# Hybrid decoder step, convolution stage: SiLU as one ScalarE function per group of four tiles, z in the last group, norms issued later

## The chip, the cores and the metric

The kernel runs on one core of one Trainium2 chip. The metric is device time in microseconds (us) of one execution; lower is better. The core has TensorE (PE, matmuls; its weight loads are listed as PEld), VectorE (DVE), ScalarE (ACT), GpSimd (POOL) and SyncE (SP, which issues most DMAs). Each engine works through its own instructions in order, and they wait for each other through semaphores.

## The reference, cut to what matters

One layer of a decoder on 256 prompt rows and 32 sample rows (288 in all). The normalised input is multiplied by `w_in`; the columns feed two attention mixers and a gated DeltaNet (mixer B). The change is in mixer B: a causal depthwise convolution of width 4 with SiLU on q, k and v, a normalisation of q and k, and a SiLU gate z at the output.

```python
def delta_branch(b_qkv, b_z, b_beta, b_alpha, conv_buf, s0, conv_w, a_log, dt_bias, dn_g):
    full = jnp.concatenate([conv_buf.astype(b_qkv.dtype), b_qkv], axis=1)
    conv = sum(full[:, j:j + L] * conv_w[j] for j in range(CONV_W))
    conv = jax.nn.silu(conv).astype(jnp.float32).reshape(n, L, 3, B_HEADS, B_HEAD_DIM)
    q = l2_normalize(conv[:, :, 0]) * (B_HEAD_DIM ** -0.5)
    k = l2_normalize(conv[:, :, 1])
    v = conv[:, :, 2]
    ...
    o, s_new = gated_delta_chunked(q, k, v, g, beta, s0)
    o = rms_norm(o, dn_g) * jax.nn.silu(b_z.astype(jnp.float32).reshape(n, L, B_HEADS, B_HEAD_DIM))
```

Then `x + norm(mix @ w_out)`, and an MLP with `w_up` and `w_down`.

## The kernel before, in words

Activations lie transposed: features on the 128 partitions, the 288 rows along the free axis. Every weight matrix is a stream of **pieces**, in a fixed order: 88 of `w_in` and one small one (`w_ba`), 32 of `w_out`'s first part (o1), 8 of its second (o2), then the MLP's. A `w_in` piece is 128x1024, that is eight 128x128 blocks; two pieces make one unit of 128 output columns. fp32 accuracy is had from three FP32R products: the weight is split into a high half `wh` and a low half `wl`, the activation into `xh` and `xl`, and each block costs three matmuls of 288 columns (`run_mats`, L447, all recorded at L307), so 24 for a `w_in` piece and 18 for an o1 piece (six blocks). Per piece SP loads the raw weight `wr`, ACT casts it to `wh` (`split_to`, L366, recorded at L375), and DVE subtracts `wl = wr - wh` (`low_to`, L385, recorded at L317). For a piece with the mark `gp`, set at L1381 for six pieces of mixer B, POOL does that subtraction. Casts are issued four pieces ahead of the matmuls, subtractions three, loads six; there are four buffers each of `wr`, `wh` and `wl`.

The last 24 pieces of `w_in` give the twelve **convolution tiles** m = 0 to 11 (0-3 are q, 4-7 k, 8-11 v; one tile per head). The four z units come before them and wait in `mixp[:, 6:10, :]` (`base_mix` in the profile). When a tile's matmuls are done, `conv_tile` (L615) scales the accumulator into `cv_zb` with two DVE instructions. Then a generator `g_conv` (L640) is stepped: ACT multiplies by the first tap and DVE adds three taps (all writing `cv_ca`), and SiLU is built from Exp and Ln without changing the activation table. `silu_a` or L653 clamps (DVE, writes `cv_e`), `silu_e` does Exp, Ln, Exp (ACT, `cv_e` and `cv_s`), `silu_b` does two DVE instructions (`cv_e`, `cv_s`) and a product on POOL into `cv_ca`. For q and k there follows a norm: ACT squares (`cv_sq`), PE sums over partitions with a matrix of ones (`ps_lx<-cv_sq`), ACT takes Ln and Exp (`cv_nr`) and a square, DVE makes the scale with two instructions (`cv_sq`), and POOL multiplies by `cv_nr` and by the scale (`b_k`, `b_qD`, `b_kD`). For v, PE transposes the tile (`ps_mx<-base_cst,cv_ca`) and ACT copies it to `b_vt`. `cv_sq` and `cv_nr` have two buffers each.

Such side work is woven between the matmuls. Each piece is cut in four, and after each cut `advance` (L487) steps every generator that is ready by an estimated PE clock; a generator yields how much PE time has to pass before its next step. `drain` (L514) forces a generator to its end. So the order on every engine is fixed when the program is built. `g_silu_z` (L575) makes the SiLU of the four z tiles after all convolution tiles. `g_gate` makes the decay gates (`cv_gc`, `cv_gd`, `cv_bD`, `cv_gD`). `g_chunk` (L813, two chunks of 128 rows) waits for tiles 0-7, computes `b_cA`, `b_cB`, `b_cU` from k and q, and inverts a triangular matrix by levels (`inverse`, L763: `b_cN`, `b_cM`, `b_cAA`); these products run among the o1 pieces. `g_bfin` ends the mixer before the o2 pieces. At the start of o1, `split_mix` splits twelve finished rows of the mix (ACT casts `base_xh<-base_mix`, DVE subtractions `base_xl`).

Of the kernel before, what the change touches and what calls it, by code (L numbers as in the profile page):

```python
# [7 lines left out]
AF = mybir.ActivationFunctionType  # L8
ALU = mybir.AluOpType
# [4 lines left out]
P = 128  # L14
# [3 lines left out]
T = TP + TS  # L18
# [221 lines left out]
def build(tc, d):  # L240
    nc = tc.nc
    PE, V, S, G, SP = nc.tensor, nc.vector, nc.scalar, nc.gpsimd, nc.sync
# [23 lines left out]
    def mx(n=512, p=P):  # L266
        return ps.t([P, 512], "mx", 4)[0:p, 0:n]
# [17 lines left out]
    dng = pm[:, 112:113]  # L285
# [23 lines left out]
    def tr(out, in_, idn):  # L309
        clk[0] += max(in_.shape[0], in_.free_size()) / 600.0  # L310
        PE.transpose(out, in_, idn)  # L311

    def act(out, in_, func, **kw):
        S.activation(out=out, in_=in_, func=func, **kw)  # L314

    def tt(eng, out, a, b, op):
        eng.tensor_tensor(out=out, in0=a, in1=b, op=op)  # L317

    def ts(eng, out, a, s1, op0, s2=None, op1=None):
        if op1 is None:  # L320
            eng.tensor_scalar(out=out, in0=a, scalar1=s1, scalar2=None, op0=op0)
        else:
            eng.tensor_scalar(out=out, in0=a, scalar1=s1, scalar2=s2, op0=op0, op1=op1)

    def stt(eng, out, a, s, b, op0, op1, **kw):
        eng.scalar_tensor_tensor(out=out, in0=a, scalar=s, in1=b, op0=op0, op1=op1, **kw)  # L326
# [25 lines left out]
    pieces = []  # L352
# [161 lines left out]
    def drain(*names):  # L514
        guard = 0
        while any(n not in done for n in names):
            for name in [g[1] for g in sorted(gens, key=lambda g: g[2])]:
                if guard % 6 < 5 and name not in names:
                    continue
                for i in range(len(gens)):  # L520
                    if gens[i][1] == name:
                        step(i)
                        break
                if all(n in done for n in names):
                    return
            guard += 1
            assert guard < 5000, (names, [g[1] for g in gens])
# [30 lines left out]
    def open_b():  # L558
        bp.open("b", "right")
        cv.open("cv")  # L560
        cvp["buf"] = cv.t([P, 12, 24], "cbuf")
        cvp["co"] = cv.t([P, 12, 27], "convo")
        SP.dma_start(out=cvp["buf"], in_=d["cbuf"])
        B["k"], B["q"] = (bp.t([P, 4, TP], "k4", 2) for _ in range(2))
        B["vt"] = bp.t([P, 2, 4, P], "vt")
        B["kD"], B["qD"], B["vD"] = (bp.t([P, P], t) for t in ("kD", "qD", "vD"))
        B["o"] = bp.t([P, 4, T], "oB")
        add_gen(g_silu_z(), "siluz", 6.0)
        add_gen(g_gate(), "gate")
# [5 lines left out]
    def g_silu_z():  # L575
        for h in range(4):
            z = mixp[:, 6 + h, :]
            while not all(f"cs{m}" in done for m in range(12)):
                yield 3.0
            e, q = silu_a(cv, z, T)  # L580
            yield 2.0
            silu_e(e, q)
            yield 4.0
            silu_b(e, q, z, G)
            yield 2.5
            act(z, z, AF.Identity, scale=dng)
            yield 1.0

    def maybe_close_cv():
        if "sp" not in done and all(n in done for n in ["siluz", "gate", "convout"] + [f"conv{m}" for m in range(12)]):  # L590
# [5 lines left out]
    def silu_a(pool, x, w):
        e = pool.t([P, ZW], "e", 3)
        s = pool.t([P, ZW], "s", 3)
        ts(V, e[:, :w], x, -80.0, ALU.max)
        return e[:, :w], s[:, :w]  # L600

    def silu_e(e, s):
        act(e, e, AF.Exp, scale=-1.0)
        act(s, e, AF.Ln, bias=1.0, scale=1.0)
        act(s, s, AF.Exp, scale=-1.0)

    def silu_b(e, s, x, eng):
        stt(V, e, e, 1.0, s, ALU.add, ALU.mult)
        stt(V, s, e, 2.0, s, ALU.subtract, ALU.mult, reverse0=True)
        tt(eng, x, x, s, ALU.mult)  # L610

    def decv(ap):
        return ap[:, 259:315].rearrange("p (n s) -> p n s", s=7)[:, :, 0:4]

    def conv_tile(m, acc):  # L615
        if m >= 4:
            drain(f"conv{m - 4}")
        if m >= 3:
            drain(f"cz{m - 3}")
        zb = cv.t([P, ZW], "zb", 3)  # L620
        G.memset(zb[:, 0:3], 0.0)
        zd = zb[:, 259:315].rearrange("p (n s) -> p n s", s=7)
        G.tensor_copy(out=zd[:, :, 0:3], in_=cvp['buf'][:, m, :].rearrange("p (n s) -> p n s", s=3))
        R = cur["R"]
        tt(V, zb[:, 3:259], acc[:, 0:TP], R[:, 0:TP], ALU.mult)
        tt(V, zd[:, :, 3:7], acc[:, TP:T].rearrange("p (n s) -> p n s", s=4),
           R[:, TP:T].rearrange("p (n s) -> p n s", s=4), ALU.mult)
        G.tensor_copy(out=cvp['co'][:, m, 0:3], in_=zb[:, 256:259])
        G.tensor_copy(out=cvp['co'][:, m, 3:27].rearrange("p (n s) -> p n s", s=3), in_=zd[:, :, 4:7])
        add_gen(g_conv(m, zb), f"conv{m}", 1.5, front=True)  # L630
        if m == 11:
            add_gen(g_convout(), "convout")

    def g_convout():
# [2 lines left out]
            yield 2.0  # L637
        G.dma_start(out=d["conv"], in_=cvp['co'])

    def g_conv(m, zb):  # L640
        kind, h = m // 4, m % 4
        while m >= 3 and f"cs{m - 3}" not in done:
            yield 1.0
        y = cv.t([P, ZW], "ca", 5)
        yc = y[:, :CW]
        act(yc, zb[:, 0:CW], AF.Identity, scale=convw[:, m, 0:1])
        yield LT[6]
        for j in range(1, 4):
            stt(V, yc, zb[:, j:j + CW], convw[:, m, j:j + 1], yc, ALU.mult, ALU.add)
        e = cv.t([P, ZW], "e", 3)[:, :CW]  # L650
        q = cv.t([P, ZW], "s", 3)[:, :CW]
        ts(V, e, yc, -80.0, ALU.max)
        done.add(f"cz{m}")  # L653
        yield LT[0]
        silu_e(e, q)
        yield LT[1]
        silu_b(e, q, yc, G)
        done.add(f"cs{m}")
        yield LT[2] if kind < 2 else LT[8]
        if kind < 2:  # L660
            while m >= 2 and f"cn{m - 2}" not in done:
                yield 1.0
            sq = cv.t([P, ZW], "sq", 2)
            act(sq[:, :CW], yc, AF.Square)
            yield LT[3]
            p = lx(CW)
            mm(p, ones, sq[:, :CW])
            yield LT[4]
            r = cv.t([P, CW], "nr", 2)
            act(r, p, AF.Ln, bias=epsc[:, 0:1], scale=1.0)  # L670
            act(r, r, AF.Exp, scale=-0.5)
            w = sq[:, :CW]
            act(w, r, AF.Square)
            yield LT[5]
# [11 lines left out]
            done.add(f"cn{m}")
        else:
            G.tensor_copy(out=B["vD"][:, 32 * h:32 * h + 32].rearrange("p (n s) -> p n s", s=4), in_=decv(y))
            p = mx(256)
            for c in range(2):  # L690
                tr(p[:, c * P:(c + 1) * P], y[:, c * P:(c + 1) * P], ident)
            S.copy(out=B["vt"][:, :, h, :], in_=p.rearrange("p (c n) -> p c n", c=2))
# [1188 lines left out]
```

## Time and profile before

| what | us |
|---|---|
| three runs before | 1435.38, 1436.96, 1439.16 (median 1436.96) |
| the profiled execution's own time | 1436.89 |
| its span, first to last instruction | 1435.0 |
| PE busy | 1384.9 (97%) |
| DVE busy | 823.1 (57%) |
| ACT busy | 601.8 (42%) |
| POOL busy | 177.3 (12%) |
| convolution stage: first matmul after the tile-0 pieces to the first `b_cN` x `b_cAA` product | 329.42 to 445.38 |

The page gives busy times as averages over the whole span. The stage in question is about a twelfth of it, so it has to be read with views of that stretch alone: busy time per 20 us, waits by releaser, groups by shape, and the order of time. In the view of stretches, a row gives the stretch, its length, and per engine busy us and number of instructions, then the granted clock of TensorE (1.00 is full speed) and the DMA share. In the view of groups, a row ends with total busy us, mean ns of one | idle time before them and what ended it.

### The profile page before, as it was taken

What the parts mean: (1) busy time and instruction counts of PE and PEld (TensorE: products, weight loads), DVE (VectorE), ACT (ScalarE), POOL (GpSimd) and SP (SyncE); (2) the same over time, 40 slices, a digit from 0 to 9 for tenths busy, and PEclk for the clock granted to TensorE, in tenths of its full rate; (3) what the DMA queues carried; (4) which work ended last, traced back from release to release, by engine and by line L of the source; (5) the groups of instructions that cost most, each with busy time, mean ns of one, the idle gap of its engine ahead of it and who ended that gap; (6) DMA issues with size and microseconds to landing.
All of it is one profiled execution on the core that took longest, in us unless ns stands there. A gap on an engine that the chain in (4) does not pass through costs nothing.

```text
span 1435.0 us, 25761 instructions
## 1 busy us (share of the span) xinstructions
PE 1384.9 (97%) x10685; PEld 1320.9 (92%) x10685; DVE 823.1 (57%) x1313; ACT 601.8 (42%) x943; POOL 177.3 (12%) x230
## 2 busy tenths in 40 slices
PE   7899999999999998999999999999999999999994
PEld 7688888789889998899999999999999999999994
DVE  7454455437999647977534455434555444555555
ACT  7343434435664235653433343333334333344441
POOL 2112111103861005000000000000000000000114
PEclk9999999999999999999999999999999999999997
DMA  7778888753433244645554454455554554545541
GB/s 260 271 269 328 298 320 335 272 183 117 140 93 104 88 156 132 213 162 191 179 175 162 149 175 162 162 176 163 161 169 156 175 166 158 176 158 167 172 151 66
DMA packets 70629, 262.27 MB, mean 183 GB/s; under 512 B 8080, under 2 KB 10256, under 8 KB 70512
## 3 DMA queue, kind: packets, MB, share of 16 engines
q1 hardware_dynamic: 68112, 254.94, 52.6%
q0 software_dynamic: 1536, 4.89, 0.9%
q8 instruction: 84, 1.38, 0.4%
q10 hardware_dynamic: 864, 0.80, 0.2%
q14 instruction: 33, 0.27, 0.1%
HBM read 253.35 MB, written 7.24 MB: 182 GB/s over the span
## 4 chain that ended last, share of the span: by engine, by line
PE 86%; DVE 8%; DMA 2%; issue 2%; POOL 1%; ACT 1%; POOLq 0%; SPq 0%; ACTq 0%; DVEq 0%
PE ps_mx L307 34%; PE ps_acc L307 31%; PE ps_lx L307 20%; DVE base_wl L317 2%; DVE cv_ca L326 2%; PE ps_mx L311 1%; DMA kv_kv<-kv_k 1%; POOL ml_y L317 1%; DVE base_mix L317 1%; DMA base_cst<-cst 1%; DVE cv_e L326 1%; DVE base_xl L317 1%; DVE base_xl L326 0%; DVE cv_s L326 0%; DVE cv_zb L317 0%
## 5 line engine op out<-in xcount | busy, mean ns | idle before, releaser
L375 ACT CAST base_wh<-base_wr 128x1024 fp32r<-128x1024 f32 (+1 forms) x376 | 387.0, 1031 | 566.8 <-PE ps_mx L307 207.3
L317 DVE TENSOR_TENSOR base_wl<-base_wr,base_wh 128x1024 fp32r<-128x1024 f32 (+1 forms) x369 | 449.3, 1231 | 66.3 <-ACT base_wh L375 64.4
L307 PE MATMUL ps_acc<-base_xh,base_wh 128*128 128x288 f32 (+1 forms) x1056 | 325.3, 309 | 3.4 <-ACT base_xh L1476 3.4
L307 PE MATMUL ps_acc<-base_xl,base_wh 128*128 128x288 f32 (+1 forms) x1056 | 313.7, 299 | 0.4
L307 PE MATMUL ps_acc<-base_xh,base_wl 128*128 128x288 f32 x1040 | 309.6, 298 | 0.7 <-DVE base_wl L317 0.6
L307 PEld LDWEIGHTS ps_acc<-base_xh,base_wh 128*128 128x128 f32 (+1 forms) x1056 | 199.9, 189 | 20.9 <-issue 14.6
L307 PE MATMUL ps_mx<-ml_big,base_wh 128*128 128x288 f32 x1024 | 203.3, 295 | 0.0
L307 PEld LDWEIGHTS ps_acc<-base_xl,base_wh 128*128 128x128 f32 (+1 forms) x1056 | 199.5, 189 | 2.6 <-DVE base_xl L317 1.4
L307 PEld LDWEIGHTS ps_acc<-base_xh,base_wl 128*128 128x128 f32 x1040 | 198.6, 191 | 1.5 <-DVE base_wl L317 1.4
L307 PEld LDWEIGHTS ps_mx<-ml_big,base_wh 128*128 128x128 f32 x1024 | 164.3, 188 | 0.0
L307 PE MATMUL ps_mx<-ml_big,base_wl 128*128 128x288 f32 x512 | 151.1, 295 | 0.0
L307 PE MATMUL ps_mx<-base_xh,base_wh 128*128 128x288 f32 x480 | 142.5, 297 | 0.0
L307 PE MATMUL ps_mx<-base_xl,base_wh 128*128 128x288 f32 x480 | 141.9, 296 | 0.0
L307 PE MATMUL ps_mx<-base_xh,base_wl 128*128 128x288 f32 x480 | 141.4, 295 | 0.0
L307 PE MATMUL ps_lx<-base_xh,base_wh 128*128 128x288 f32 x400 | 121.2, 304 | 6.1 <-ACT base_xh L314 6.1
L307 PE MATMUL ps_lx<-base_xh,base_wl 128*128 128x288 f32 x400 | 118.7, 297 | 3.3 <-DVE base_wl L317 3.3
L307 PE MATMUL ps_lx<-base_xl,base_wh 128*128 128x288 f32 x400 | 117.8, 298 | 0.0
L307 PE MATMUL ps_lx<-ml_big,base_wh 128*128 128x288 f32 x512 | 101.8, 295 | 0.0
L307 PE MATMUL ps_acc<-ml_big,base_wh 128*128 128x288 f32 x512 | 101.8, 295 | 0.0
L317 POOL TENSOR_TENSOR ml_sacc<-ml_sacc,ml_sq 128x288 f32<-128x288 f32 x15 | 12.8, 853 | 717.3 <-ACT ml_sq L314 717.3
L307 PEld LDWEIGHTS ps_mx<-ml_big,base_wl 128*128 128x128 f32 x512 | 96.4, 188 | 0.0
L307 PEld LDWEIGHTS ps_mx<-base_xh,base_wl 128*128 128x128 f32 x480 | 90.5, 189 | 0.0
(415 smaller groups left out, 2028.6 us busy)
## 6 DMA issues: line engine op xcount, KB each, us to landing
base_wr<-w_up SPq DMA_DIRECT2D x128, 512.0 KB, 3.5
base_wr<-w_dn SPq DMA_DIRECT2D x128, 512.0 KB, 3.5
base_wr<-w_in SPq DMA_DIRECT2D x88, 512.0 KB, 4.3
kv_kv<-kv_k SPq DMA_DIRECT2D x24, 896.0 KB, 8.3
kv_kv<-kv_v SPq DMA_DIRECT2D x28, 768.0 KB, 7.1
base_wr<-w_o SPq DMA_DIRECT2D x32, 384.0 KB, 3.1
base_wr<-w_o SPq DMA_DIRECT2D x8, 512.0 KB, 4.0
ml_big<-xT SPq DMA_DIRECT2D x4, 576.0 KB, 4.8
```

What stands on the lines that cost most here:

```text
L307: PE.matmul(out, lhsT=lhsT, rhs=rhs, start=start, stop=stop, **kw)
L311: PE.transpose(out, in_, idn)
L317: eng.tensor_tensor(out=out, in0=a, in1=b, op=op)
L326: eng.scalar_tensor_tensor(out=out, in0=a, scalar=s, in1=b, op0=op0, op1=op1, **kw)
L375: S.copy(out=p["wh"], in_=p["wr"])
```

## The change

SiLU of the convolution tiles becomes one ScalarE function (`AF.Silu`). It needs another activation table, so tiles are taken in groups of four: `g_group(kind)` waits until its four tiles have all taps added, loads the table set `silu_and_others` by name, applies Silu in place to four tiles, and loads `natural_log_exp_and_others` again. In the last group (v), one Silu over all four z tiles at once (128x1152) stands ahead of the four, and one multiplication by `dng` over 1152 columns follows; `g_silu_z` goes. The norms of a group are stepped one after the other after its Silu. The norm is written another way: ACT's third square and POOL's product with `cv_nr` go, and DVE has three scalar_tensor_tensor instead of one and a tensor_scalar. `cv_ca` has nine buffers instead of five; the buffers `cv_e` and `cv_s` go. The mark `gp` at L1381 goes, so the six low halves that POOL made are DVE's.

```diff
@@ open_b: the generator of z goes
-        add_gen(g_silu_z(), "siluz", 6.0)
         add_gen(g_gate(), "gate")
...
     def conv_tile(m, acc):
-        if m >= 4:
-            drain(f"conv{m - 4}")
+        if m >= NCA:
+            while f"conv{m - NCA}" not in done:
+                drain(f"convg{(m - NCA) // 4}")
         if m >= 3:
             drain(f"cz{m - 3}")
...
-        add_gen(g_conv(m, zb), f"conv{m}", 1.5, front=True)
+        add_gen(g_conv(m, zb), f"convt{m}", 1.5, front=True)
+        if m % 4 == 3:
+            add_gen(g_group(m // 4), f"convg{m // 4}", 1.5, front=True)
...
+    NCA = 9
+
     def g_conv(m, zb):
-        kind, h = m // 4, m % 4
-        while m >= 3 and f"cs{m - 3}" not in done:
-            yield 1.0
-        y = cv.t([P, ZW], "ca", 5)
+        y = cv.t([P, ZW], "ca", NCA)
+        cvp["y", m] = y
         yc = y[:, :CW]
         act(yc, zb[:, 0:CW], AF.Identity, scale=convw[:, m, 0:1])
         yield LT[6]
         for j in range(1, 4):
             stt(V, yc, zb[:, j:j + CW], convw[:, m, j:j + 1], yc, ALU.mult, ALU.add)
-        e = cv.t([P, ZW], "e", 3)[:, :CW]
-        q = cv.t([P, ZW], "s", 3)[:, :CW]
-        ts(V, e, yc, -80.0, ALU.max)
         done.add(f"cz{m}")
-        yield LT[0]
-        silu_e(e, q)
-        yield LT[1]
-        silu_b(e, q, yc, G)
...
+    def g_group(kind):
+        ms = range(4 * kind, 4 * kind + 4)
+        while not all(f"cz{m}" in done for m in ms):
+            yield 1.0
+        yield 1.5
+        S.preload_act_table_set("silu_and_others")
+        if kind == 2:
+            zs = mixp[:, 6:10, :]
+            act(zs, zs, AF.Silu)
+        for m in ms:
+            yc = cvp["y", m][:, :CW]
+            act(yc, yc, AF.Silu)
+        S.preload_act_table_set("natural_log_exp_and_others")
+        if kind == 2:
+            act(zs, zs, AF.Identity, scale=dng)
+            done.add("siluz")
+        yield 6.0
+        for m in ms:
...
             sq = cv.t([P, ZW], "sq", 2)
             act(sq[:, :CW], yc, AF.Square)
-            yield LT[3]
+            yield 2.5
             p = lx(CW)
             mm(p, ones, sq[:, :CW])
-            yield LT[4]
             r = cv.t([P, CW], "nr", 2)
             act(r, p, AF.Ln, bias=epsc[:, 0:1], scale=1.0)
             act(r, r, AF.Exp, scale=-0.5)
             w = sq[:, :CW]
-            act(w, r, AF.Square)
-            yield LT[5]
             sc = float(P) ** -0.5 if kind == 0 else 1.0
-            stt(V, w, p, EPS, w, ALU.add, ALU.mult)
-            ts(V, w, w, -0.5 * sc, ALU.mult, 1.5 * sc, ALU.add)
-            tt(G, yc, yc, r, ALU.mult)
-            yield LT[7]
+            stt(V, w, p, EPS, r, ALU.add, ALU.mult)
+            stt(V, w, w, -0.5 * sc, r, ALU.mult, ALU.mult)
+            stt(V, w, w, 1.5 * sc, r, ALU.add, ALU.mult)
             dp, dd = ((B["q"], B["qD"]), (B["k"], B["kD"]))[kind]
             tt(G, dp[:, h, :], y[:, 0:TP], w[:, 0:TP], ALU.mult)
...
-            pieces[-1]["gp"] = u != "ba" and UNITS[u][0] == "b" and u % 2 == 0 and h == 0
```

The change moves instructions at three places that matter below. First POOL, in the stretch where the norms of q are made (`b_k_2` here is the q buffer). Before:

```order
L317 TENSOR_TENSOR cv_ca_3929<-cv_ca_3929,cv_s_3973 128x312
L317 TENSOR_TENSOR base_wl_4062<-base_wr_3912,base_wh_4061 128x1024
L621 MEMSET cv_zb_4102 128x3
L623 COPY cv_zb_4102<-cv_cbuf_3688 128x8x3
L628 COPY cv_convo_3689<-cv_zb_4102 128x3
L629 COPY cv_convo_3689<-cv_zb_4102 128x24
L317 TENSOR_TENSOR cv_ca_3828<-cv_ca_3828,cv_nr_4074 128x312
L317 TENSOR_TENSOR b_k_2_3692<-cv_ca_3828,cv_sq_4031 128x256
L317 TENSOR_TENSOR b_qD_3695<-cv_ca_3828,cv_sq_4031 128x28
L317 TENSOR_TENSOR b_qD_3695<-cv_ca_3828,cv_sq_4031 128x4
```

POOL there after the change:

```order
L317 TENSOR_TENSOR b_k_2_3691<-cv_ca_3743,cv_sq_4148 128x256
L317 TENSOR_TENSOR b_qD_3694<-cv_ca_3743,cv_sq_4148 128x28
L317 TENSOR_TENSOR b_qD_3694<-cv_ca_3743,cv_sq_4148 128x4
L591 MEMSET cv_zb_4216 128x3
L593 COPY cv_zb_4216<-cv_cbuf_3687 128x8x3
L598 COPY cv_convo_3688<-cv_zb_4216 128x3
L599 COPY cv_convo_3688<-cv_zb_4216 128x24
```

Of POOL's work per q tile only the products with the scale and the small copies are left; the 1024-column subtraction and two 312-column products are gone.

Second, DVE in the same stretch. Before:

```order
L326 SCALAR_TENSOR_TENSOR cv_e_4081<-cv_e_4081,cv_s_4082 128x312
L326 SCALAR_TENSOR_TENSOR cv_s_4082<-cv_e_4081,cv_s_4082 128x312
L326 SCALAR_TENSOR_TENSOR cv_ca_4146<-cv_zb_4102,base_pm_62,cv_ca_4146 128x312 x3
L321 TENSOR_SCALAR cv_e_4176<-cv_ca_4146 128x312
L317 TENSOR_TENSOR cv_zb_4197<-ps_acc_4114,base_R_387 128x256
L317 TENSOR_TENSOR cv_zb_4197<-ps_acc_4114,base_R_387 128x8x4
L317 TENSOR_TENSOR base_wl_4155<-base_wr_4022,base_wh_4154 128x1024
L326 SCALAR_TENSOR_TENSOR cv_sq_4124<-ps_lx_4144,cv_sq_4124 128x312
L323 TENSOR_SCALAR cv_sq_4124<-cv_sq_4124 128x312
L317 TENSOR_TENSOR base_wl_4205<-base_wr_4066,base_wh_4204 128x1024
```

DVE there after the change:

```order
L317 TENSOR_TENSOR base_wl_4096<-base_wr_3987,base_wh_4095 128x1024
L317 TENSOR_TENSOR base_wl_4136<-base_wr_4020,base_wh_4135 128x1024
L326 SCALAR_TENSOR_TENSOR cv_sq_4148<-ps_lx_4182,cv_nr_4184 128x312
L326 SCALAR_TENSOR_TENSOR cv_sq_4148<-cv_sq_4148,cv_nr_4184 128x312 x2
L326 SCALAR_TENSOR_TENSOR cv_ca_4162<-cv_zb_4128,base_pm_62,cv_ca_4162 128x312 x3
L317 TENSOR_TENSOR cv_zb_4216<-ps_acc_4141,base_R_387 128x256
L317 TENSOR_TENSOR cv_zb_4216<-ps_acc_4141,base_R_387 128x8x4
L317 TENSOR_TENSOR base_wl_4171<-base_wr_4066,base_wh_4170 128x1024
```

The clamp and the two SiLU instructions are gone, the norm has three instructions, and every piece's low half stands here. Norms now follow each other every 24 weight matmuls instead of every 48, and the first four begin five tiles later.

Third, ACT among the first o1 pieces, where the last group lies. `b_cT` belongs to the second chunk's gates, `b_vt` are the transposed v tiles, `b_cAA` the copies for the inversion. Before:

```order
L314 ACTIVATE b_cT_27_4827<-b_cT_27_4827 128x512
L692 COPY b_vt_3693<-ps_mx_4904 128x2x128
L375 CAST base_wh_4908<-base_wr_4756 128x768
L314 ACTIVATE cv_e_4883<-cv_e_4883 128x312
L314 ACTIVATE cv_s_4884<-cv_e_4883 128x312
L314 ACTIVATE cv_s_4884<-cv_s_4884 128x312
L375 CAST base_wh_4956<-base_wr_4833 128x768
L692 COPY b_vt_3693<-ps_mx_5000 128x2x128
L771 COPY b_cAA_32_5010<-ps_mx_5013 128x512
```

ACT there after the change:

```order
L314 ACTIVATE b_cT_27_4733<-b_cT_27_4733 128x512
L375 CAST base_wh_4803<-base_wr_4660 128x768
L629 ACT_TABLE_LOAD
L314 ACTIVATE base_mix_65<-base_mix_65 128x1152
L314 ACTIVATE cv_ca_4437<-cv_ca_4437 128x312
L314 ACTIVATE cv_ca_4512<-cv_ca_4512 128x312
L314 ACTIVATE cv_ca_4605<-cv_ca_4605 128x312
L314 ACTIVATE cv_ca_4751<-cv_ca_4751 128x312
L636 ACT_TABLE_LOAD
L314 ACTIVATE base_mix_65<-base_mix_65,base_pm_62 128x1152
L375 CAST base_wh_4853<-base_wr_4739 128x768
L650 COPY b_vt_3692<-ps_mx_4897 128x2x128
```

Two table loads, five Silu and the scaling of z stand as one block between two casts, ahead of all four `b_vt` copies. SP's order is unchanged, and PE's is the same again from the first `b_cN` x `b_cAA` product on.

More of the change, by code (lines that the diff above doesn't have):

```diff
@@ L573, in open_b @@
         add_gen(g_bfin(), "bf")
[L575 to L581, printed above, removed]
-            silu_e(e, q)
[L583 to L586, printed above, removed]
-            yield 1.0
     def maybe_close_cv():
@@ L594, in maybe_close_cv @@
             done.add("sp")
[L596 to L610, printed above, removed]
     def decv(ap):
@@ L638, in g_convout @@
         G.dma_start(out=d["conv"], in_=cvp['co'])
+    NCA = 9
     def g_conv(m, zb):
-        kind, h = m // 4, m % 4
-        while m >= 3 and f"cs{m - 3}" not in done:
-            yield 1.0
-        y = cv.t([P, ZW], "ca", 5)
+        y = cv.t([P, ZW], "ca", NCA)
+        cvp["y", m] = y
         yc = y[:, :CW]
@@ L649, in g_conv @@
             stt(V, yc, zb[:, j:j + CW], convw[:, m, j:j + 1], yc, ALU.mult, ALU.add)
-        e = cv.t([P, ZW], "e", 3)[:, :CW]
-        q = cv.t([P, ZW], "s", 3)[:, :CW]
-        ts(V, e, yc, -80.0, ALU.max)
         done.add(f"cz{m}")
-        yield LT[0]
-        silu_e(e, q)
-        yield LT[1]
-        silu_b(e, q, yc, G)
[L658 to L662, printed above, removed]
+    def g_group(kind):
[16 more added lines that the diff above has]
+        for m in ms:
+            h = m % 4
+            y = cvp.pop(("y", m))
+            yc = y[:, :CW]
+            if kind == 2:
+                G.tensor_copy(out=B["vD"][:, 32 * h:32 * h + 32].rearrange("p (n s) -> p n s", s=4), in_=decv(y))
+                p = mx(256)
+                for c in range(2):
+                    tr(p[:, c * P:(c + 1) * P], y[:, c * P:(c + 1) * P], ident)
+                S.copy(out=B["vt"][:, :, h, :], in_=p.rearrange("p (c n) -> p c n", c=2))
+                done.add(f"conv{m}")
+                yield 0.7
+                continue
             sq = cv.t([P, ZW], "sq", 2)
             act(sq[:, :CW], yc, AF.Square)
-            yield LT[3]
+            yield 2.5
             p = lx(CW)
             mm(p, ones, sq[:, :CW])
-            yield LT[4]
             r = cv.t([P, CW], "nr", 2)
@@ L685, in g_conv @@
             tt(G, dv_[:, 7, :], yv[:, 7, :], sq[:, 308:312], ALU.mult)
[L686 to L692, printed above, removed]
+            done.add(f"conv{m}")
+        yield 2.5
     def g_gate():
```

## The prediction

> **What bounds the kernel now.** I read the page's totals first, then busy time per 20 us, then TensorE's waits in the stage, then the groups behind the engine that makes PE wait.
>
> ```profile
> PE 1384.9 (97%) x10685; PEld 1320.9 (92%) x10685; DVE 823.1 (57%) x1313; ACT 601.8 (42%) x943; POOL 177.3 (12%) x230
> 340.00:360.00 20.00, 18.43 (x121) 17.57 (x121) 17.55 (x35) 12.52 (x25) 11.33 (x17) 0.91 0.41 132
> 360.00:380.00 20.00, 17.88 (x119) 17.36 (x118) 19.58 (x28) 13.18 (x24) 16.79 (x23) 0.91 0.40 132
> ...
> 420.00:440.00 20.00, 18.51 (x138) 17.09 (x138) 19.72 (x45) 12.95 (x33) 5.25 (x7) 1.00 0.31 99
> ...
> 460.00:480.00 20.00, 20.00 (x169) 20.00 (x168) 14.06 (x25) 5.11 (x8) 1.34 (x2) 1.00 0.27 80
> ```
>
> PE is busy 97% of the span, so a gain has to come from the places where it is not. The convolution stage is one: PE is idle 1.5 to 2.1 us of every 20, and there DVE, 57% on average, is busy 19.6 and 19.7 of 20. At 460:480 PE is full again. The work on z before it lies at 440 to 460, so its end delays nobody; taking it away is worth nothing at that place.
>
> ```profile
> engine line waited for: us in total, times, longest us
> PE ps_lx L307 <- ACT cv_sq L314: 5.7, 3, 2.5
> PE ps_mx L307 <- POOL cv_bD L720: 1.4, 1, 1.4
> ...
> ```
>
> These are PE's waits from 329 to 446; with five more, 2.2 together and none over 0.6, they sum to 9.3. To them comes the clock: 0.91 in two stretches means 0.09 x 20 = 1.8 us lost in each, 3.6 in all. So **12.9 us** lie in this stage (a count of its matmuls at 0.133, worked out below, gives about 14.7). The largest wait is for the squares of the norm, which stand late because the chain DVE taps, SiLU, POOL product ends late.
>
> **DVE's load.** Why is DVE full?
>
> ```profile
> L326 DVE SCALAR_TENSOR_TENSOR cv_ca<-cv_zb,base_pm,cv_ca 128x312 f32<-128x312 f32 x36 | 33.1, 919 | 1.4 <-ACT cv_ca L314 0.6
> L326 DVE SCALAR_TENSOR_TENSOR cv_ca<-cv_zb,base_pm,cv_ca x36: 534/545/3023, 336.8 to 431.6; 128x312 f32<-128x312 f32 x36
> 361.99 4.33 DVE L326 SCALAR_TENSOR_TENSOR cv_ca<-cv_zb,base_pm,cv_ca 128x312 f32<-128x312 f32 x3
> 362.74 2.65 POOL L317 TENSOR_TENSOR base_wl<-base_wr,base_wh 128x1024 fp32r<-128x1024 f32 x1
> 430.43 1.70 DVE L326 SCALAR_TENSOR_TENSOR cv_ca<-cv_zb,base_pm,cv_ca 128x312 f32<-128x312 f32 x3
> ```
>
> The taps' median is 545 ns (minimum, median, maximum in the second row), their mean 919: three of them take 4.33 us while POOL subtracts a low half beside them, and 1.70 at 430.43, where POOL has nothing. So 36 x (919 - 545) = 13.5 us of DVE's time go with POOL's work beside it.
>
> **What goes and comes on DVE.**
>
> ```profile
> L326 DVE SCALAR_TENSOR_TENSOR cv_e<-cv_e,cv_s 128x312 f32<-128x312 f32 x12 | 9.5, 790 | 0.0
> L326 DVE SCALAR_TENSOR_TENSOR cv_s<-cv_e,cv_s 128x312 f32<-128x312 f32 x12 | 5.8, 485 | 0.4
> L321 DVE TENSOR_SCALAR cv_e<-cv_ca 128x312 f32<-128x312 f32 x12 | 3.9, 322 | 0.4
> L323 DVE TENSOR_SCALAR cv_sq<-cv_sq 128x312 f32<-128x312 f32 x8 | 6.5, 807 | 0.3
> L326 DVE SCALAR_TENSOR_TENSOR cv_sq<-ps_lx,cv_sq 128x312 f32<-128x312 f32 x8 | 3.8, 474 | 0.0
> L317 DVE TENSOR_TENSOR base_wl<-base_wr,base_wh 128x1024 fp32r<-128x1024 f32 x15 | 18.2, 1214 | 0.0
> ```
>
> Clamps and SiLU's two steps leave: 3.9 + 9.5 + 5.8 = 19.2. The norm goes from 0.474 + 0.807 to three of 0.474 = 1.42: plus 0.14 x 8 = 1.1. Six low halves come back: 6 x 1.21 = 7.3. Of the 13.5 most goes with POOL's low halves and SiLU products; some 2 to 3 us stay beside POOL's `b_k` products. In sum DVE loses 19.2 - 1.1 - 7.3 + 11 = about 22 us in a stage of five slices of at most 20 each. It has room again at every piece until the last group.
>
> **ACT.**
>
> ```profile
> L314 ACT ACTIVATE cv_e<-cv_e 128x312 f32<-128x312 f32 x12 | 5.6, 465 | 19.0 <-DVE cv_e L321 19.0
> L1734 ACT ACT_TABLE_LOAD x1 | 1.3, 1283 | 0.7 <-PEq L1871 0.7
> L314 ACT ACTIVATE sp_fa<-b_oB 128x1152 f32<-128x1152 f32 x1 | 1.2, 1172 | 0.0
> ```
>
> 36 functions of 0.465 become 12; eight squares go. No Silu is in this trace: the nearest rows are Exp (0.465) and the taps' Identity (0.545), and I take 0.47, by the shape of Exp. Over 1152 columns one function takes 1.17; z needs two. [...] ACT is busy 12.5 to 13.2 of 20 us in the slices above, so four of the six loads, behind which only casts issued four pieces ahead wait, cost nothing; without that cover they would cost 1.3 each. The two of the v group do not hide, as the sum shows.
>
> [...]
>
> **PE's way to the chunk's matrices.** From the first product of `b_cN` and `b_cAA` on, the orders of before and after are the same and PE is full, so what counts is when that product stands.
>
> ```profile
> 326.00 0.29 PE L307 MATMUL ps_acc<-base_xh,base_wl 128*128 128x288 f32 x1
> ...
> 329.20 0.29 PE L307 MATMUL ps_acc<-base_xh,base_wl 128*128 128x288 f32 x1
> 375.33 0.79 PE L307 MATMUL ps_lx<-cv_sq,base_cst 128*128 128x312 f32 x2 [2.12 <-ACT cv_sq L314]
> 419.03 1.95 PE L307 MATMUL ps_mx<-base_cst,b_gP 128*128 128x128 f32 x16
> 445.38 1.05 PE L307 MATMUL ps_mx<-b_cN,b_cAA 128*128 128x128 f32 x8
> ```
>
> 24 matmuls later is 3.20 us later: 0.133 each. The gate products `b_gP` stood at 419.03. Lost until then: 5.7 for `cv_sq`, 1.4 for `cv_bD` and 3.6 of clock, 10.7 in all. If nothing of it stays (the waits go with DVE's load; the half clock followed such waits), they stand at 408.3. The sum over partitions of the first k norm (tile 4) stands 72 matmuls (9.6) and four norm sums (0.7 each) ahead of them: at about 395.9. So Ln and Exp have its scale ready at about 397.5.
>
> **DVE's tail** has no gap from there, in the new order:
>
> ```profile
> 416.90 3.67 DVE L317 TENSOR_TENSOR base_xl<-base_mix,base_xh 128x288 fp32r<-128x288 f32 x8
> ...
> 422.23 0.51 DVE L317 TENSOR_TENSOR cv_zb<-ps_acc,base_R 128x256 f32<-128x256 f32 x2
> 422.66 1.56 DVE L317 TENSOR_TENSOR base_xl<-base_mix,base_xh 128x288 fp32r<-128x288 f32 x4
> 427.48 0.15 DVE L825 COPY b_gl<-ps_mx 128x4 f32<-128x4 f32 x1
> ...
> 429.56 0.95 DVE L317 TENSOR_TENSOR base_wl<-base_wr,base_wh 128x768 fp32r<-128x768 f32 x1
> 437.55 0.68 DVE L317 TENSOR_TENSOR b_cB<-ps_mx,b_cA 128x512 f32<-128x512 f32 x1
> 438.15 1.11 DVE L326 SCALAR_TENSOR_TENSOR b_cU<-ps_mx,b_bP,b_cA 128x128 f32<-128x128 f32 x4
> ```
>
> Four k norms 5.7; one low half of 1024 columns 1.2; six of 768 (0.9 to the next start) 5.4; taps of tiles 9 to 11, 5.1 and 1.0 beside `b_k`; two `cv_zb` 1.0; `base_xl` 5.2; from `b_gl` to the `wl` behind it 2.1, and 0.5 for that group's start; `b_cB` and `b_cU` twice 3.4; a copy 0.4. Sum 31.0: the second `b_cU` ends at about **428.5**, against 439.26 now.
>
> ```profile
> 428.97 1.26 ACT L314 ACTIVATE b_cA<-b_cA,b_ngc 128x128 f32<-128x128 f32 x4
> ...
> 432.94 0.35 ACT L692 COPY b_vt<-ps_mx 128x256 f32<-128x256 f32 x1
> ```
>
> ACT's leg: its work from the first `b_cA` to `b_cT` takes 4.0 us (428.97 to 432.94). Shifted with DVE's `b_cA` rows it starts at 418.8; a cast of 0.8 behind it ends at 423.6. Then load 1.28, Silu over z 1.17, Silu of tile 8 0.47: 426.5. PE stands at tile 8's transposes for about 2 us, since its in-order queue has them ahead of the transposes of `b_cU`. Both legs then end alike: PE has some 3.3 us of transposes and small products (the first behind 426.5), to 429.8; 36 matmuls (4.8) and 0.5 of small ones, and the product stands at 435.1. **Gain 10.3.** I deduct 1.3: a half clock of 1.8 after the new waits at even odds (0.9), and 0.4 for change-overs dearer than the row. So 9.0 from the profiled run's own 1436.89 (its median of three is 1436.96): **1428**; own range 1425 to 1432.
>
> The clock rows of 0.91 follow waits of only 1.4 and 2.1 us. [...]
>
> **POOL** loses 12 products and six low halves, which no PE wait names, and keeps `b_k` and `b_qD`:
>
> ```profile
> 358.49 1.58 POOL L317 TENSOR_TENSOR b_k<-cv_ca,cv_sq 128x256 f32<-128x256 f32 x1 [0.32 <-DVE cv_sq L323]
> 360.04 0.96 POOL L317 TENSOR_TENSOR b_qD<-cv_ca,cv_sq 128x28 f32<-128x28 f32 x2
> ```
>
> **The rivals.**
> *PE-bound throughout (0.13).* DVE's tail and the Silu group are shorter than I add them up, all 12.9 to 14.7 us come back: 1422 to 1424. For it: 97% PE. Against: DVE 19.72 of 20 us at 420:440, where nothing but SiLU's steps leaves.
> *A dearer tail (0.14).* [...]
> *The long taps stay (0.12).* The 13.5 us are not POOL's removed work: `b_k`, bunched, blocks DVE as much. Then DVE's load falls by only 11, the stage keeps about two thirds of its loss: gain 3 to 4, 1433. Against it: the pair at 361.99 and 362.74.
> *Slower (0.09): the norm's ring.* Norms now come one behind the other, one for about each piece (3.2 + 0.7 us), on two `cv_sq` buffers. One buffer's round is 0.45 square + 0.8 sum + 1.0 Ln and Exp + 1.4 DVE + 2.5 POOL = 6.2 us, against two slots of 7.8. It decides when DVE or POOL reaches a norm over 1.5 us late; then PE waits for `cv_sq` at each of eight norms as at 375.33, 2.1 x 8 = 17, and 5 in the tail: 22 against 14.7 lost now, +7: 1444. Against it: DVE has room there.
>
> **How the numbers follow.** The forecast has 0.52. About 0.3%, 4.3 us, is what a measurement can tell from no change, so faster means below 1432.6: 0.52 + 0.13 + 0.09 of the dearer tail = 0.74. Within: its other 0.05 and the long taps, 0.17. Slower 0.09. The range runs from the PE-bound end to the long taps, 1421.5 to 1434.5, and leaves the ring and some of each end out.
>
> **What would show it.** Right: `cv_ca` taps at a mean of 0.55 to 0.65; PE's waits for `cv_sq` under 0.5; clock 1.00 from 340 to 380; seven table loads of 1.28; the `b_cN` product at about 435; a wait of about 2 us at tile 8's transposes for ACT's `cv_ca`. From there all rows shifted alike. Wrong: `cv_sq` waits at each norm (ring); taps still near 0.9; a clock below 1.00 in 420:440; or idle in front of ACT's functions beyond the load.

## The result, and the profile after

| | before | after |
|---|---|---|
| median (runs) | 1437.43 us (4) | 1427.66 us (4) |
| lowest and highest | 1435.38 to 1439.16 | 1425.44 to 1428.06 |
| profiled execution, its span | 1436.89, 1435.0 | 1427.82, 1426.0 |

The ratio is 0.9924, with a 95% interval of 0.9912 to 0.9936: 9.8 us faster by the medians, 9.0 by the two spans. The forecast was 1428.0.

First the totals of the kernel after, and its busy time per 20 us in the stage (columns as before: stretch, length, then busy us and instructions of PE, PEld, DVE, ACT and POOL, granted clock, DMA share, GB/s).

```profile
PE 1380.8 (97%) x10685; PEld 1317.3 (92%) x10685; DVE 798.1 (56%) x1279; ACT 590.7 (41%) x903; POOL 138.7 (10%) x200
340.00:360.00 20.00, 20.00 (x153) 19.82 (x153) 14.87 (x32) 9.95 (x17) 8.35 (x14) 1.00 0.59 197
360.00:380.00 20.00, 20.00 (x147) 19.56 (x146) 14.96 (x26) 13.37 (x21) 8.72 (x16) 1.00 0.40 133
380.00:400.00 20.00, 20.00 (x149) 19.70 (x148) 16.41 (x29) 14.35 (x22) 7.69 (x18) 1.00 0.46 138
400.00:420.00 20.00, 19.14 (x138) 18.00 (x137) 19.65 (x44) 12.83 (x32) 9.95 (x20) 1.00 0.25 80
420.00:440.00 20.00, 17.70 (x140) 17.00 (x139) 16.98 (x32) 15.27 (x28) 3.62 (x7) 1.00 0.33 93
```

From 340 to 400 PE is full at full clock, and DVE has 3.6 to 5.1 us of every 20 to spare. What is left of the loss lies behind 400, in the tail: there DVE is full again, and then PE has its largest gaps, 2.3 us of 20. PE's waits from 329 to 437 in the kernel after say the same:

```profile
PE ps_lx L307 <- DVE base_wl L317: 0.8, 1, 0.8
PE ps_mx L311 <- ACT cv_ca L314: 0.8, 1, 0.8
PE ps_acc L307 <- DVE base_xl L317: 0.7, 1, 0.7
PE ps_mx L311 <- ACT b_vt L650: 0.7, 1, 0.7
PE ps_acc L307 <- DVE base_wl L317: 0.5, 1, 0.5
```

3.5 us in place of 9.3; no wait for `cv_sq` or `cv_bD`. **A measure for the stage**: runs differ by some us before it starts, since PE waits at 40 us for the DMA of `kv_k` (the longest of these waits is 5.0 us in the kernel after, and 3.7 in e9 below). So I read it between two products that every kernel here has, the gate's and the first of `b_cN` with `b_cAA`. In order of time, in the kernel after:

```profile
329.97 0.65 PE L307 MATMUL ps_mx<-base_R,base_cst 16*8 16x288 f32 x2
...
435.72 1.05 PE L307 MATMUL ps_mx<-b_cN,b_cAA 128*128 128x128 f32 x8
```

435.72 - 329.97 = **105.75**; before it was 445.38 - 329.42 = **115.96**. The stage is 10.2 us shorter. The spans differ by 9.0, since this execution reached the stage 0.55 later and lost another 0.7 between the o1 and o2 pieces, where waits for `base_xl` of that size stand that the kernel before did not have. The start differs from run to run. The 0.7 comes with the kernel: from the first `b_cN` x `b_cAA` product to the end it takes 989.6 us before, 990.3 after, and 990.5 in a second profile of the kernel after (e10 below), with the same kind of wait.

The end of the stage, from the chain of waits of the kernel after (start, length in us, engine and what it writes), shows which engine it goes through:

```profile
417.05 0.48 DVE cv_sq L326
417.61 0.61 DVE b_cA L317
...
420.34 1.28 ACT b_cA L314 x4
421.81 0.52 ACT b_cT L314
422.33 0.72 ACT base_wh L375
423.06 1.28 ACT L629
424.36 1.17 ACT base_mix L314
425.58 0.20 issue
425.78 1.16 ACT cv_ca L314 x3
426.96 1.28 ACT L636
428.25 1.26 ACT base_mix L314
429.51 0.72 ACT base_wh L375
430.23 0.27 ACT b_vt L650
430.50 0.49 ACT b_cAA L753
431.02 0.70 DVE b_cM L317
...
433.77 0.88 DVE base_wl L317
434.69 1.19 PE ps_lx L307 x7
435.88 1.34 PE ps_mx L307 x12
```

From 418 to 431 it is ACT without a break: table load (L629), z's Silu, the four tiles, load (L636), z's scale, a cast, two copies. DVE's second `b_cU` was over at 427.84. So ACT's leg ends last, not both alike.

### The profile page after: what moved, and what is told of

Same layout as the page of the kernel before. It is cut to its first block, busy times and chain, and to the rows that moved or that the text cites. A ratio compares the mean times of both kernels' runs of the same rounds, so it can differ in the third digit from the quotient of the medians.

```text
span 1426.0 us, 25678 instructions
## 1 busy us (share of the span) xinstructions
PE 1380.8 (97%) x10685; PEld 1317.3 (92%) x10685; DVE 798.1 (56%) x1279; ACT 590.7 (41%) x903; POOL 138.7 (10%) x200
## 3 DMA queue, kind: packets, MB, share of 16 engines
q8 instruction: 84, 1.38, 0.4%
## 4 chain that ended last, share of the span: by engine, by line
PE 90%; DVE 4%; DMA 2%; ACT 2%; POOL 1%; issue 1%; SPq 0%; POOLq 0%; DVEq 0%; ACTq 0%
PE ps_acc L307 34%; PE ps_mx L307 34%; PE ps_lx L307 20%; PE ps_mx L311 1%; DMA kv_kv<-kv_k 1%; POOL ml_y L317 1%; DVE base_wl L317 1%; DMA base_wr<-w_in 1%; DVE base_mix L317 1%; DMA base_cst<-cst 1%; DVE base_xl L326 0%; ACT base_xh L1457 0%; DVE cv_sq L326 0%; DVE x_sa L317 0%; DVE base_xl L317 0%
## 5 line engine op out<-in xcount | busy, mean ns | idle before, releaser
L317 DVE TENSOR_TENSOR base_wl<-base_wr,base_wh 128x1024 fp32r<-128x1024 f32 (+1 forms) x375 | 456.3, 1231 | 67.2 <-ACT base_wh L375 67.1
L307 PEld LDWEIGHTS ps_acc<-base_xh,base_wh 128*128 128x128 f32 (+1 forms) x1056 | 198.0, 188 | 21.3 <-issue 15.1
L307 PEld LDWEIGHTS ps_mx<-base_xl,base_wh 128*128 128x128 f32 x480 | 90.1, 188 | 0.1
```

The costliest lines, as they stand in the source:

```text
L307: PE.matmul(out, lhsT=lhsT, rhs=rhs, start=start, stop=stop, **kw)
```

## The experiments

Times are medians in us; each ratio is to runs of the kernel before that were taken beside it (their medians lie from 1437.28 to 1438.05); the stage is read as above, from each kernel's own profile.

| kernel | median (runs) | its ratio to before, 95% | gate's product | first `b_cN` x `b_cAA` | stage |
|---|---|---|---|---|---|
| before | 1437.43 (4) | | 329.42 | 445.38 | 115.96 |
| after | 1427.66 (4) | 0.9912 to 0.9936 | 329.97 | 435.72 | 105.75 |
| e1 POOL's low halves back | 1425.45 (5) | 0.9911 to 0.9936 | 329.57 | 434.91 | 105.34 |
| e3 z in the first group | 1427.45 (5) | 0.9917 to 0.9942 | 331.47 | 435.56 | 104.09 |
| e4 two more loads | 1429.08 (5) | 0.9933 to 0.9960 | 328.55 | 437.64 | 109.09 |
| e5 one `cv_sq` buffer | 1442.85 (5) | 1.0031 to 1.0056 | 329.83 | 450.72 | 120.89 |
| e2 before, low halves on DVE | 1435.76 (12) | 0.9973 to 0.9994 | 330.74 | 444.53 | 113.79 |
| e6 before, norm rewritten | 1439.34 (12) | 0.9998 to 1.0017 | 331.25 | 448.57 | 117.32 |
| e8 SiLU in groups alone | 1426.90 (6) | 0.9906 to 0.9934 | 328.88 | 434.05 | 105.17 |
| e7 e1 and e3 together | 1426.48 (6) | 0.9902 to 0.9932 | 332.71 | 437.10 | 104.39 |
| e9 e3 with the old norm | 1425.57 (5) | 0.9896 to 0.9923 | 330.63 | 434.64 | 104.01 |
| e10 after again | 1427.22 (5) | 0.9913 to 0.9938 | 330.15 | 435.90 | 105.75 |
| e11 e3 again | 1426.05 (4) | 0.9904 to 0.9931 | 330.98 | 435.07 | 104.09 |

### Does the measure repeat? (e10, e11)

No edit: the changed kernel, and the kernel of e3, once more.

> The changed kernel once more, unchanged, to see how well the stage and the median repeat beside kernels of the same call. If the stage is set by the program and the starts differ by chance, the stage is 105.75 within 0.1 and the start of the stage differs from 329.97 by up to 2 us; if not, differences of some tenths between stages above mean nothing.

> The changed kernel with z in the first group once more, beside the changed kernel itself in the same call. If its stage is shorter by 1.66 and nothing gives it back, its median is 1 to 2 us below the changed kernel's; if a later wait takes it back, equal medians.

The stages come out at 105.75 and 104.09 again, equal to 0.01, while the gate's product stood anywhere from 328.55 to 332.71 over all kernels. So tenths of the stage can be read, and medians that are less than about 2 us apart cannot be ranked. The stage is not the whole effect, though: behind it, the kernels differ by up to 1.3 us (989.2 to 989.8 in e1, e2, e4, e6 and e8, 990.2 to 990.5 in e3, e5, e7, e9, e10 and e11). The median of e11 is 1.2 below that of e10, as its stage says, but the intervals overlap.

### Which edit made the gain? (e8, e2, e6, e1)

**e8**: of the change only SiLU in groups (with z and the buffers). To the changed kernel:

```diff
+            pieces[-1]["gp"] = u != "ba" and UNITS[u][0] == "b" and u % 2 == 0 and h == 0
...
             w = sq[:, :CW]
+            act(w, r, AF.Square)
...
-            stt(V, w, p, EPS, r, ALU.add, ALU.mult)
-            stt(V, w, w, -0.5 * sc, r, ALU.mult, ALU.mult)
-            stt(V, w, w, 1.5 * sc, r, ALU.add, ALU.mult)
+            stt(V, w, p, EPS, w, ALU.add, ALU.mult)
+            ts(V, w, w, -0.5 * sc, ALU.mult, 1.5 * sc, ALU.add)
+            tt(G, yc, yc, r, ALU.mult)
```

> The changed kernel with the old norm and with POOL's low halves back, so that of the change only SiLU as one function in groups (with z and nine cv_ca buffers) is left. Theory A (SiLU's 19.2 us of DVE work and its 12 POOL products are the change; the two other edits only shift work): stage 105 to 107, as the changed kernel. Rival B (the norm's shorter round is needed as soon as norms follow one another): PE waits for cv_sq at the second to fourth norm of each group, since the round grows by 0.47 + 0.85 to about 6.5 against 3.9 between norms of two buffers, 7.8 for both: 1.0 to 2 us of waits at some of them, stage 108 to 112.

105.17: all of the gain and 0.6 more than the whole change (1.3 more up to the end of the kernel, as the waits for `base_xl` behind the stage are not there either). There is no wait for `cv_sq`, so the shorter norm was not needed for the ring. This edit still holds several things together: the 19.2 us that leave DVE, the 12 products that leave POOL, and the later place of the norms. No run takes these apart. Its taps are still long at places (group of the stage, in e8: total, mean ns):

```profile
L326 DVE SCALAR_TENSOR_TENSOR cv_ca<-cv_zb,base_pm,cv_ca 128x312 f32<-128x312 f32 x36 | 27.1, 753 | 1.7 <-ACT cv_ca L314 0.9
340.00:360.00 20.00, 20.00 (x153) 19.82 (x153) 16.72 (x29) 9.92 (x17) 10.18 (x16) 1.00 0.54 168
```

but with 16.7 of 20 us DVE has room for them, and PE is full.

**e2**: the kernel before, with only the mark gone.

```diff
-            pieces[-1]["gp"] = u != "ba" and UNITS[u][0] == "b" and u % 2 == 0 and h == 0
```

> The kernel before with only the mark gp taken away: its six low halves go from POOL to DVE. I read the stage from the gate's product (ps_mx<-base_R) to the first b_cN x b_cAA product, 115.96 in the kernel before and 105.75 in the changed one, since the starts of the runs differ by up to 2 us. Theory A (four of these POOL rows each stretched one tap by 2.0 to 2.5 us, 8.6 in all, and DVE pays 6 x 1.21 = 7.3 for them instead): DVE's sum hardly changes, the taps' mean falls from 0.919 to about 0.68 (the POOL SiLU products stay, 0.48 each), and the stage falls by 0 to 3 us: 113 to 116. Rival B (the long rows were what made the norms late): the stage falls by 5 or more, to 110. Rival C (DVE is full, 7.3 more on it delays): it rises by 2 or more.

Theory A holds: the stage falls by 2.2 (PE's waits for `cv_sq` go from 5.7 to 3.5, and one of the two half-clock stretches is gone), and the group of taps in e2 reads

```profile
L326 DVE SCALAR_TENSOR_TENSOR cv_ca<-cv_zb,base_pm,cv_ca 128x312 f32<-128x312 f32 x36 | 24.5, 680 | 0.8
```

33.1 - 24.5 = 8.6 us less, just what was worked out for the four rows that stood beside POOL's low halves. So the stretching of these four rows is caused by POOL's low halves. DVE stays at 19.5 to 19.6 of 20 from 360 to 420, since the six low halves are now its own.

**e6**: the kernel before, with only the norm rewritten (the reverse of the norm lines of e8's diff).

> The kernel before with only the norm rewritten: ACT's third square and POOL's product with cv_nr go, DVE has three steps of 0.48 instead of 0.474 + 0.807. Theory A (the waits for cv_sq come from DVE's queue, not from the norm's own chain): DVE gets 1.1 us more in all, the ring loses 0.47 on ACT and 0.85 on POOL per norm, and the stage changes by less than 2: 114.5 to 117. Rival B (PE's 5.7 us of waits for cv_sq were the ring of two buffers, which is 1.2 us shorter now): the waits fall by more than half and the stage falls by 3 to 5, to 112.

117.32, 1.4 longer, just outside theory A's 117 on its slow side; B falls (6.6 us of waits for `cv_sq` against 5.7). So the rewrite gains nothing in the kernel before. Its three steps take 11.5 us on DVE (eight times 0.474 + 2 x 0.483), against 10.2 before, 1.3 more, which is near the 1.4; that this is the reason is argued and not shown.

**e1**: the changed kernel with the mark back (the first line of e8's diff).

> The changed kernel with POOL's six low halves back (the mark gp), all else as changed. Compare with 1427.7. Theory A (a POOL subtraction of 2.6 us beside a row of three taps lengthens it by about 2 us, so POOL's low halves cost DVE more than the 1.21 us that they save): the taps' mean rises from 0.598 to about 0.85 (6 x 1.5 to 2 us over 36 taps), DVE's busy time per 20 us from 340 to 400 rises from 15 to about 17, which its idle time there takes up, and only what falls behind tile 4's norm is paid: +0 to +2 us, 1428 to 1430. Rival B (the low halves on POOL are what made PE wait before, so that most of the gain is theirs): PE waits for cv_sq or wl again and the time goes up by 5 or more, to 1433. Rival C (the long taps had another cause): the mean stays below 0.65, DVE gets 7 us freer and the time falls to 1426.

The taps' mean goes up to 0.727, less than the 0.85 of theory A, as only two taps met such a row. One of DVE's own low halves met one too and took 3.43 us instead of 1.22 (the mean of those 128x1024 rows is 1.39, against 1.24 in the kernel after), and PE waited for it by no more than 0.1. The stage is 0.4 shorter, not longer: what is missing is the wait of 0.5 for a low half at its head (at 338.00, the last row of the waits of after). The direction of A's price was wrong; none of the three got both numbers.

Together: 115.96 goes to 113.79 with the low halves alone, to 117.32 with the norm alone, to 105.17 with SiLU alone, and to 105.75 with all three. Singly they sum to 11.6, together they give 10.2. Beside SiLU in groups the two other edits gain nothing and cost 0.6; that SiLU's steps have already freed DVE there fits the rows, but is argued.

### What ends the stage? (e3, e4, e7, e9)

**e3**: z in the first group. PE, DVE and POOL keep their order.

```diff
-        if kind == 2:
+        if kind == 0:
             zs = mixp[:, 6:10, :]
             act(zs, zs, AF.Silu)
...
-        if kind == 2:
+        if kind == 0:
             act(zs, zs, AF.Identity, scale=dng)
```

> The changed kernel with the Silu over z and its scale in the first group (q) instead of the last; the order on PE, DVE and POOL is the same, on ACT only these two of 1.17 and 1.26 us move. Theory A (ACT's row in the last group, load, z, four Silu, load, z's scale, cast, b_vt, b_cAA, is what the first b_cN x b_cAA product waits for, DVE's second b_cU at 427.8 being close behind): tile 8 ready 1.2 earlier, b_cAA copied 2.2 earlier, PE's waits of 0.8 at tile 8, 0.7 for b_vt and 0.8 for a low half behind b_cM go: the product 1.5 to 2.3 earlier, about 1425.8. Rival B (DVE's tail ends last, as the prediction had it beside ACT's leg): under 0.6 gained, 1427.2. Rival C: in the first group z pushes the norms of q back and PE waits there, slower by 1 or more.

The stage is 1.66 shorter, within theory A's 1.5 to 2.3, and the norms of q did not suffer (PE is full from 340 to 400). PE's waits in e3 have lost the one for `cv_ca` and the one for a low half behind `b_cM`:

```profile
PE ps_mx L311 <- ACT b_vt L650: 1.0, 1, 1.0
PE ps_acc L307 <- DVE base_xl L317: 0.7, 1, 0.7
PE ps_acc L307 <- DVE base_wl L317: 0.5, 1, 0.5
```

The median of e3 is only 0.2 below the changed kernel's; its runs spread from 1425.04 to 1428.14, so this says nothing against the stage. e11 against e10 shows 1.2.

**e4**: two more loads behind the first of the last group.

```diff
         S.preload_act_table_set("silu_and_others")
         if kind == 2:
+            S.preload_act_table_set("natural_log_exp_and_others")
+            S.preload_act_table_set("silu_and_others")
```

> The changed kernel with two more table loads (to the other set and back) right behind the first load of the last group. Nothing else moves. Theory A (a change-over costs the load's 1.28 us and no more, and the path runs through ACT): two rows of 1.28 without idle time between them, +2.6 on ACT, +2.3 to 2.6 on the time, 1430.1. [...] Rival C (ACT's leg has slack beside DVE's): under +1.

109.09, 3.34 longer. In e4, PE's wait for tile 8 and the stretch around it read:

```profile
PE ps_mx L311 <- ACT cv_ca L314: 3.4, 1, 3.4
420.00:440.00 20.00, 16.65 (x113) 16.40 (x112) 14.45 (x28) 15.95 (x25) 3.49 (x7) 0.83 0.28 88
```

and ACT's rows there, in order of time:

```profile
421.71 1.28 ACT L629 ACT_TABLE_LOAD   x1
423.00 1.28 ACT L631 ACT_TABLE_LOAD   x1
424.28 1.28 ACT L632 ACT_TABLE_LOAD   x1
425.58 1.16 ACT L314 ACTIVATE base_mix<-base_mix 128x1152 f32<-128x1152 f32 x1
```

The loads follow one another within 0.02 us. The wait grew from 0.8 to 3.4, by the two loads' 2.57 and no more: ACT's leg has no slack, and nothing beyond their rows came with the loads. The later waits for `b_vt` and for the low half, 1.5 together, are gone, and 3.34 - 2.6 + 1.5 = 2.2 are left. The clock can account for them: it was half from 426.2 to 433.0 (0.83 in the stretch above), and PE worked again from 427.2 on. Behind the stage e4 gives 0.9 back, so that up to the end it is 2.4 longer than the changed kernel, as theory A had it; the medians differ by 1.4.

**e7** puts e1 and e3 together, **e9** is e3 with the old norm (the norm lines of e8's diff).

> The changed kernel with z in the first group and POOL's low halves back, the two single edits that shortened the stage (to 104.09 and 105.34 from 105.75). Theory A (independent: one frees ACT in the tail, the other DVE at the pieces before): about 103.7, and the time by some 2 us below the changed kernel's median, 1425.5. Rival B (in the tail DVE's sum is what is left and POOL's rows block it there): 104.1 or more, no gain over z alone.

> The changed kernel with z in the first group and with the old norm (ACT's third square, DVE 0.474 + 0.807, POOL's product with cv_nr); POOL's low halves stay off. Theory A (the old norm is shorter on DVE by 0.14 us each, DVE's tail is what is left once z is gone): the stage falls from 104.09 to 103.4 to 103.9. Rival B (POOL's 0.85 us product and ACT's square make each norm later, and the cv_sq ring is on the tail's chain): 104.3 or more.

104.39 and 104.01, against 104.09 with z alone. For e7 rival B has the number, but not the place: the wait of 0.5 at the head is gone, and a new one of 0.8 stands at 393.56, before the tail. There one of DVE's own low halves (390.07) took 3.43 us instead of 1.22, beside POOL's of 2.64 at 389.78. e9 lies between its two theories and tells nothing apart. Once z is out of the tail, 1.7 us of waits are left there, for `base_xl` and for the copy `b_vt` (the 0.5 for a low half is at the head), and no edit tried here removed them. e3, e11 and e9 are the ones that beat the changed kernel in the stage by more than 1.6. e9 has the lowest ratio of the kernels tried, 0.9909, but its interval overlaps that of the changed kernel.

### Does the ring of `cv_sq` decide? (e5)

```diff
-            sq = cv.t([P, ZW], "sq", 2)
+            sq = cv.t([P, ZW], "sq", 1)
```

> The changed kernel with one cv_sq buffer instead of two; the order on every engine is the same. It tests the ring of the slower rival. Its round, from rows of after: square 0.46, sum over partitions 0.54, Ln and Exp 1.0, three DVE steps 1.48, POOL products 1.4 to 2.0: 4.9 to 5.5 us, against 3.9 between two norms. Theory A (the ring decides once its round is longer than the slots): PE waits for cv_sq at the second to fourth norm of each group, 1.0 to 1.6 each, 6 to 10 in all, of which the tail takes 3 to 5 through the k norms: 1431 to 1436. Rival B (norms are further apart than a piece, or DVE's slack takes it up): same within 1, 1427 to 1428.5.

The mechanism of theory A holds, and its size was too small: 15.1 us on the stage, and slower than the kernel before. In e5:

```profile
PE ps_lx L307 <- ACT cv_sq L314: 11.0, 6, 3.6
380.00:400.00 20.00, 15.85 (x95) 15.11 (x96) 12.39 (x21) 11.94 (x19) 6.09 (x17) 0.83 0.28 84
400.00:420.00 20.00, 17.35 (x112) 16.44 (x111) 11.63 (x20) 8.42 (x16) 5.97 (x12) 0.91 0.31 95
```

Six waits, one for the second to the fourth norm of both groups, as the theory has it, of 1.8 on average; and the clock, 0.83 and 0.91, which costs about 0.17 x 20 + 0.09 x 20 = 5.2 more, an estimate. With two buffers there is no such wait at all.

## Why the prediction was right, point by point

**What bounds, and the loss of 12.9.** Right: the waits that were named went, and so did both half-clock stretches (1.00 from 340 on).

**DVE's load.** Taken as 22 us less; the page has 823.1 - 798.1 = 25.0, and that holds z's steps too, 4.8, which were left out; the terms that were counted come to 21.7 in the rows of after. The taps' mean is 0.598, inside 0.55 to 0.65, and what stays beside `b_k` is 36 x (598 - 544) = 1.9 us, taken as 2 to 3. The rows were read rightly, and e2 shows the cause. But the step that counted them all towards the gain was wrong in one thing: 8.6 us for POOL's low halves, less 7.3 for doing them on DVE, is nearly nothing, and e8 and e1 show that the changed kernel does not need it. The 0.807 of the old norm's second step, taken as its cost, was not its own either: in the kernel before, each of the eight ended 0.18 us after POOL's `cv_nr` product beside it, and in e8, with the same norm, three of them had no product beside them and took 0.32.

**ACT.** Silu takes 0.45 (0.47 taken), over z 1.17, and the six loads 1.283 each. A function follows a load within 0.02 us (423.06 + 1.28, then 424.36), and e4's two more loads follow within 0.02 us too. Four of the loads were hidden, as forecast: from 340 to 400 PE has no wait.

**PE's way and the tail.** The times forecast and found:

| event | forecast | after |
|---|---|---|
| `b_gP` products | 408.3 | 408.76 |
| first k norm's scale ready | 397.5 | 398.5 |
| second `b_cU` ends | 428.5 | 427.8 |
| ACT's first `b_cA` | 418.8 | 418.2 |
| first load of the v group | 423.6 | 423.06 |
| tile 8 ready | 426.5 | 425.9 |
| first `b_cN` x `b_cAA` | 435.1 | 435.72 |

The gain up to that product was taken as 10.3 and is 9.7, and 10.2 between the two marks. That the second `b_cU` came out right joins two errors: the tail on DVE began 1.0 later, and its sum was 29.3 and not 31.0. **The step that failed in detail** is "Both legs then end alike": DVE's leg ended before ACT's and waited. Behind tile 8 I followed PE's own matmuls, but the path stayed on ACT through the second load and z's scale to `b_cAA`, and DVE's `b_cM` waited 2.8 us for it; PE's wait at tile 8 was 0.8 and not 2, and 1.5 came later (`b_vt`, and a low half behind `b_cM`). Two errors of opposite sign that left the sum alone. e3 and e4 show the leg from both sides.

**The deduction of 1.3** had no ground: the clock is 1.00 at 420:440, and no run shows its 0.4 for change-overs: none was dearer than its row of 1.28. That the forecast meets the median to 0.3 is thus partly luck: 0.55 at the start, in this profile, and the 0.7 between o1 and o2, which the forecast did not have, stood in its place.

**The rivals.** PE-bound throughout: no, 3.5 us of waits are left. A dearer tail: no, and no run shows a change-over that costs more than its row of 1.28; but e4 shows how it would have come, with the half clock (0.83 at 420:440) behind a wait of 3.4. The long taps stay: no, by their mean of 0.598, and e2 shows the cause. The ring: not with two buffers; e5 shows that the place was right, and that its price with one buffer (15.1 on the stage) has the clock in it.

## What to carry to other kernels

Between two instructions that all versions share, a stage can be read to a tenth of a us where the medians of runs differ by 2; with that measure, take the edits of a change one at a time: of three that were put together here, one made the whole gain, and the two others cost 0.6 of the stage beside it. Then read what lies behind the stage too, since part of a gain can be lost there (0.7 here). When an engine becomes free, look for the end of its stage in the chain of the next engine: here it was ACT's work that had been bundled into the last group although its inputs (z) had long been ready.

## What the runs showed of the hardware that was not expected

**DVE beside POOL.** In the single records of the kernels before and after, a tap that began while one of POOL's low halves, SiLU products or `b_k` products ran ended 0.34 to 0.35 us after it: in the kernel before, the four taps beside a low half, whatever it took (2.36 to 2.70), lasted 2.57 to 3.02, and those beside SiLU products 1.0 to 1.1; in the kernel after, those beside `b_k` 0.9 to 1.0; all instead of 0.55. Eight taps of the kernel before that had begun 0.1 to 0.2 us ahead of the product took 0.54 as ever, and the tap behind each of them ended 0.34 after it (one tap did so though it had begun 0.3 us ahead of the low half). DVE's own low halves were longer too: 1.62 instead of 1.22 at 383.13 in the kernel after, beside `b_k` and `b_qD`, and one of 3.43 each in e1 and e7, where their means are 1.39 and 1.38. The norm's first step was not: 0.48 at 406.00 in the kernel after, beside a `b_k` that took 1.32 and had run for 0.7 us.

**The half clock.** In the stage it came after waits of 1.4 and 2.1 us in the kernel before, but not after the longest there (2.5); in e5, whose longest wait is 3.6, the clock was 0.83 and 0.91 in two stretches of 20 us. So in the kernel before the length of a wait alone does not decide. Between 60 and 600 us the half-clock stretches of the kernel before begin at 345.77, 376.49 and 557.40 and last 3.41, 3.41 and 6.83 us, and the one of the kernel after begins at 549.28 and lasts 6.83. The second and third in the kernel before begin 9 and 62 times 3.41 us after the first. Taken in steps of 3.41 us from the first, the kernel before reads (stretch, length, then as above):

```profile
373.08:376.49 3.41, 1.29 (x9) 1.02 (x8) 3.34 (x8) 2.95 (x6) 2.33 (x4) 1.00 0.14 29
376.49:379.90 3.41, 3.41 (x17) 3.41 (x16) 3.34 (x5) 1.51 (x4) 3.41 (x4) 0.50 0.32 125
...
396.97:400.38 3.41, 2.24 (x17) 2.01 (x16) 3.34 (x6) 0.52 (x2) 2.73 (x6) 1.00 0.42 89
400.38:403.80 3.42, 2.11 (x14) 1.97 (x15) 3.35 (x5) 3.36 (x7) 3.10 (x5) 1.00 0.51 189
403.80:407.21 3.41, 3.41 (x28) 3.41 (x27) 3.31 (x8) 2.20 (x5) 2.13 (x5) 1.00 0.30 106
```

The wait of 2.1 falls into one of these windows, in which PE is idle for 2.1 us, and half clock follows. The wait of 2.5 is split into 1.2 and 1.3, and none follows. Taken in the same way from 60 to 600 us, the full-clock windows of the kernels before and after that half clock followed have 1.42 (with the 8-column products at `cv_bD`), 2.12 and 2.83 us of idle PE before, and 2.79 after; all others have at most 1.31. An earlier one, at 38.57 in the kernel before, has 1.59, and full clock followed. What decides is not shown.
